# Building gate tables: one multiplication goes to GpSimd, a third of the one-hot rows to VectorE

## The chip, the core and the metric

One core of one Trainium2 chip runs the whole layer in one launch. The metric is the device time of an execution in microseconds; the median of three runs is quoted. The engines are TensorE (PE, with its weight loads as PEld), VectorE (DVE), ScalarE (ACT), GpSimd (POOL) and SyncE (SP, which issues most of the transfers).

## The reference, cut

The kernel computes one layer over 512 tokens of width 1024. An attention group and an RWKV group come first and take the first half of the time; then comes PEER, a product-key retrieval over 128 x 128 = 16,384 single-neuron experts. For each token and each of 8 heads it picks 16 experts, each named by two keys (i1, i2), with a softmax gate:

```python
def block(hb):                       # 128 tokens
    ...
    idx = jnp.take_along_axis(cand_i, pos, axis=-1)          # i1 * 128 + i2
    gate = jax.nn.softmax(top_s, axis=-1).astype(hb.dtype)
    u = expert_u[idx]
    act = jax.nn.gelu(jnp.einsum('thkd,td->thk', u, hb), approximate=False)
    vv = expert_v[idx]
    return jnp.einsum('thk,thkd->td', gate * act, vv)
```

## The kernel before

The 512 tokens are four blocks of 128. Two of them (`GATHERED`, blocks 0 and 3) compute PEER by gathering: in `experts` each of the 128 choices of a token fetches a row of `expert_u` and one of `expert_v` by an indirect DMA that GpSimd issues (L996, 512 KB each), into four buffers `ga`. VectorE takes the dot product (L1006) or accumulates (L1009).

The other two blocks (`DENSE`, 1 and 2, together 256 tokens) compute PEER densely: `dense` goes over all 16,384 experts in 128 tiles. `up` loads a tile of `expert_ut` and multiplies it by the tokens (whole at L1133, or split in two parts and multiplied three times at L1147), with a GELU behind it; `down` multiplies the result by the gate of each token and expert (L1164) and by the tile of `expert_v` (L1168, L1185) into `po`, which stays in PSUM over all 128 tiles.

For this every token needs its gates as a 128 x 128 table over (i2, i1). `make_gates` builds these tables ahead of the loop, in 32 groups of eight tokens. `slots` holds i1, i2 and the gate, the choice (8 heads x 16) on the partitions and the token along the row. Per group:

- `B` (128 x 8 x 128): VectorE compares `iotap` (0 to 127) with i1, which gives one-hot rows (L1061), and multiplies them in place by the gate (L1062).
- `A`, of the same size: one-hot rows of i2. ScalarE computes |i2 - iotap| for each of eight tokens (L1065) and then relu(1 - that) over all eight (L1066).
- TensorE multiplies `A` by `B`, token by token (L1074), into `pg` in PSUM. ScalarE copies a part of it to `G` (L1077), which stays in SBUF, and the rest to `away` (L1078), which SP writes to DRAM every second group.

`B` has two buffers, shared with the later split `xh`, `xl`; `A` has two of its own; `pg` has four. Between two groups the loop in `dense` issues the first tiles of `up`, 16 of them over the 32 groups.

The order on the engines is not that of the source text. A planner with a model of the instructions' times (`schedule_with_timeline_sim=True` at the launch) fills each engine's queue, taking the ready instruction that comes first in the program. So the gates stage runs beside the retrieval of the last block (`back`, `retrieve`, `route`) and beside the gathered rows of `experts`, which stand last in the program and fill in. Once laid out, the order on each engine is fixed, and an instruction waits there for what it needs.

Of the kernel before, what the change touches and what calls it, by code (L numbers as in the profile page):

```python
# [13 lines left out]
AF = mybir.ActivationFunctionType  # L14
OP = mybir.AluOpType
# [3 lines left out]
P = 128  # L19
# [70 lines left out]
def layer_kernel(ctx: ExitStack, tc: tile.TileContext, x, pos, cvec, rvec, w_mla, w_rwkv, w_uq, w_ukv, lora, g2,  # L90
# [20 lines left out]
    mm, act, V, G = nc.tensor.matmul, nc.scalar.activation, nc.vector, nc.gpsimd  # L111
# [26 lines left out]
    def cst(shape, name, dt=F32, pool=pre):  # L138
        return pool.tile(shape, dt, name=name)
# [108 lines left out]
    iotap = cst([P, P], "iotap", pool=con)  # L248
# [14 lines left out]
    for j in range(16):  # L263
# [5 lines left out]
                    op=OP.mult)  # L269
# [26 lines left out]
    def bc(ap, n):  # L296
        return ap[:, :, None].to_broadcast([ap.shape[0], ap.shape[1], n])

    def bm(ap, n):
        return ap[:, None, :].to_broadcast([ap.shape[0], n, ap.shape[1]])  # L300
# [755 lines left out]
    def make_gates(dn, psd, held, far):  # L1056

        i1T, i2T, gT = slots
        for t0 in range(0, nd, 8):
            B = dn.tile([P, D], F32, tag="x", name=f"B{t0}", bufs=XB).rearrange("p (a b) -> p a b", a=8)  # L1060
            V.tensor_tensor(B, bm(iotap, 8), bc(i1T[:, t0:t0 + 8], P), op=OP.is_equal)  # L1061
            V.tensor_tensor(B, B, bc(gT[:, t0:t0 + 8], P), op=OP.mult)  # L1062
            A = dn.tile([P, 8, P], F32, tag="A", name=f"A{t0}", bufs=2)
            for j in range(8):
                act(A[:, j, :], iotap, AF.Abs, scale=-1.0, bias=i2T[:, t0 + j:t0 + j + 1])  # L1065
            act(A, A, AF.Relu, scale=-1.0, bias=1.0)  # L1066
            i = t0 % 16
            if i == 0:
                away = dn.tile([P, D], F32, tag="v", name=f"away{t0}", bufs=VB)
                away = away.rearrange("p (s t i) -> p s t i", s=P // SUB - HELD, i=SUB)  # L1070
            for h in range(2):
                p = psd.tile([P, 512], F32, tag="po", name=f"pg{t0}{h}", bufs=2 * len(DENSE))
                for j in range(4):
                    mm(p[:, j * P:(j + 1) * P], A[:, 4 * h + j, :], B[:, 4 * h + j, :], start=True, stop=True)  # L1074
                p4 = p.rearrange("p (t s i) -> p s t i", t=4, i=SUB)
                t = t0 + 4 * h
                act(held[:, :, t:t + 4, :], p4[:, :HELD], AF.Copy)  # L1077
                act(away[:, :, t % 16:t % 16 + 4, :], p4[:, HELD:], AF.Copy)  # L1078
            if i:
                nc.sync.dma_start(far[:, t0 // 16], away)  # L1080
            yield

    def dense():
# [110 lines left out]
        for i, _ in enumerate(make_gates(dn, psd, held, far)):  # L1194
            for e in range(FIRST + i * rest // n, FIRST + (i + 1) * rest // n):
                up(e, e >= AHEAD)
# [126 lines left out]
```

## Time and profile before

| | |
|---|---|
| median of three runs | 1761.57 us (1759.91, 1761.57, 1781.8) |
| profiled execution | 1773.46 us |
| its span, first to last instruction | 1771.7 us, mean granted TensorE clock 0.926 |
| PE / PEld busy | 1556.0 us (88%) / 1319.3 us (74%) |
| DVE busy | 1358.6 us (77%) |
| ACT busy | 808.1 us (46%) |
| POOL busy | 777.8 us (44%) |
| DMA | 537.52 MB, mean 303 GB/s |

Busy times are sums over the span of one execution. A busy PE is not a PE at its peak, since matrix multiplications are pipelined and their ends are modelled. In rows of instructions, "out<-in" are the program's names without buffer numbers, then partitions x elements and type. A "<-" behind a time of idleness names what ended it; "issue" means that the engine waited for nothing that the profile shows.

### The profile page before, as it was taken

The page shows a single profiled execution, that of the slowest core. Times are in us where ns is not written, and L with a number is a line of the kernel's source. Part 1 is how long each engine was busy: PE and PEld are TensorE (multiplying, and loading weights), DVE is VectorE, ACT ScalarE, POOL GpSimd, SP SyncE. Part 2 cuts the span into 40 slices and gives each one's busy share as a digit, 9 for nine tenths or more (in the row PEclk, how much of TensorE's full clock was granted, in tenths as well). Part 3 has the DMA queues.
Part 4 walks back from the last instruction along what each step waited for, and adds up shares of the span by engine and source line. Part 5 has one row for each costly group of instructions (what it writes and reads, how often), then busy time and mean ns, then how long its engine had stood idle before and what let it go on. Part 6 is the DMA issues. An engine that isn't in the chain of part 4 may idle for free. (4 is left out here: it accounts for less than half of the span.)

```text
span 1771.7 us, 29597 instructions
## 1 busy us (share of the span) xinstructions
PE 1556.0 (88%) x10803; PEld 1319.3 (74%) x10803; DVE 1358.6 (77%) x2788; ACT 808.1 (46%) x2007; POOL 777.8 (44%) x560
## 2 busy tenths in 40 slices
PE   7999998998799897789995668999969999899992
PEld 6896797876575686569985436788868888888872
DVE  3422435678886689988999857898879899898896
ACT  5645634455423422237798302444425444344440
POOL 1001100546674644454437644454445365464574
PEclk9999998998669889899997889999989999999997
DMA  8545644798889889889996899899999999999997
GB/s 279 187 140 189 228 160 129 273 362 275 300 303 385 297 312 322 311 319 359 377 308 209 314 318 347 335 360 345 350 324 367 347 334 364 348 350 364 331 340 274
DMA packets 165617, 537.52 MB, mean 303 GB/s; under 512 B 17824, under 2 KB 32800, under 8 KB 165472
## 3 DMA queue, kind: packets, MB, share of 16 engines
q0 software_dynamic: 73728, 268.47, 42.4%
q1 hardware_dynamic: 91744, 267.17, 42.2%
q8 instruction: 85, 1.39, 0.3%
q14 instruction: 60, 0.49, 0.1%
HBM read 517.34 MB, written 18.22 MB: 302 GB/s over the span
## 5 line engine op out<-in xcount | busy, mean ns | idle before, releaser
L996 POOL DMA_INDIRECT ga<-in_expert_v_dram,idx x235 | 375.8, 1599 | 315.5 <-DVE acc L1009 205.6
L996 POOL DMA_INDIRECT ga<-in_expert_u_dram,idx x225 | 287.5, 1278 | 312.8 <-DVE ga L1006 244.2
L1009 DVE SCALAR_TENSOR_TENSOR acc<-ga,dots,acc 128x1024 f32<-128x1024 f32 x235 | 300.5, 1279 | 33.3 <-DMA ga<-in_expert_v_dram,idx 32.8
L1006 DVE SCALAR_TENSOR_TENSOR ga<-ga,h 128x1024 f32<-128x1024 f32 x225 | 273.6, 1219 | 29.8 <-DMA ga<-in_expert_u_dram,idx 29.1
L1147 PE MATMUL ps<-dh,uh 128*128 128x256 f32 x800 | 231.7, 290 | 24.8 <-ACT uh L1094 24.8
L1147 PE MATMUL ps<-dh,ul 128*128 128x256 f32 x800 | 231.9, 290 | 13.4 <-DVE ul L1095 13.4
L1147 PE MATMUL ps<-dl,uh 128*128 128x256 f32 x800 | 230.5, 288 | 0.0
L1185 PE MATMUL po<-xh,t 128*128 128x512 f32 x544 | 186.1, 402 | 16.1 <-ACT xh L1094 16.1
L1147 PEld LDWEIGHTS ps<-dh,uh 128*128 128x128 f32 x800 | 157.0, 196 | 32.1 <-ACT uh L1094 27.4
L1147 PEld LDWEIGHTS ps<-dh,ul 128*128 128x128 f32 x800 | 156.7, 196 | 19.6 <-DVE ul L1095 17.1
L1147 PEld LDWEIGHTS ps<-dl,uh 128*128 128x128 f32 x800 | 156.8, 196 | 3.1 <-issue 0.5
L1185 PE MATMUL po<-x2h,t 128*128 128x512 f32 x408 | 135.3, 392 | 2.0 <-ACT x2h L1094 2.0
L1094 ACT ACTIVATE xh<-v 128x1024 fp32r<-128x1024 f32 x68 | 71.9, 1057 | 136.3 <-DMA v<-in_expert_v_dram 61.7
L1095 DVE TENSOR_TENSOR ul<-u,uh 128x1024 fp32r<-128x1024 f32 x100 | 121.9, 1220 | 13.6 <-ACT uh L1094 13.5
L1185 PEld LDWEIGHTS po<-xh,t 128*128 128x128 f32 x544 | 101.8, 192 | 39.6 <-ACT xh L1094 19.5
L844 PE MATMUL ps<-h2T,wst 128*128 128x128 f32 (+1 forms) x768 | 125.2, 319 | 4.2 <-DMA wst<-in_w_pq_dram 2.9
L1094 ACT ACTIVATE uh<-u 128x1024 fp32r<-128x1024 f32 x100 | 104.8, 1051 | 43.2 <-DMA u<-in_expert_ut_dram 33.2
L844 PEld LDWEIGHTS ps<-h2T,wst 128*128 128x128 f32 x768 | 110.8, 197 | 12.8 <-DMA wst<-in_w_pq_dram 2.2
L353 PE MATMUL ps<-hT,wst 128*128 128x129 f32 x896 | 110.8, 277 | 0.6 <-ACT t L311 0.6
L1185 PE MATMUL po<-xl,t 128*128 128x512 f32 x272 | 109.8, 404 | 0.7 <-DVE xl L1095 0.5
L1133 PE MATMUL ps<-t,u 128*128 128x256 f32 x448 | 108.0, 395 | 2.7 <-DMA u<-in_expert_ut_dram 2.0
L353 PEld LDWEIGHTS ps<-hT,wst 128*128 128x128 f32 x896 | 105.3, 191 | 6.3 <-issue 1.3
(423 smaller groups left out, 3132.6 us busy)
## 6 DMA issues: line engine op xcount, KB each, us to landing
u<-in_expert_ut_dram SPq DMA_DIRECT2D x128, 512.0 KB, 6.8
v<-in_expert_v_dram SPq DMA_DIRECT2D x128, 512.0 KB, 6.1
wst<-in_w_rwkv_dram SPq DMA_DIRECT2D x56, 512.0 KB, 4.4
wst<-in_w_pq_dram SPq DMA_DIRECT2D x48, 512.0 KB, 6.6
wst<-in_w_o_dram SPq DMA_DIRECT2D x24, 512.0 KB, 6.2
far<-away SPq DMA_DIRECT2D x16, 512.0 KB, 6.1
G<-far SPq DMA_DIRECT2D x16, 512.0 KB, 12.0
wst<-in_w_mla_dram SPq DMA_DIRECT2D x16, 336.0 KB, 6.5
```

Of the source, the lines that this page charges most:

```text
L353: mm(p[:, :P + 1], w[:, kc, :], hT[:, kc, :], start=kc == 0, stop=kc == KC - 1)
L844: mm(p[:, :nb * P], w[:, kc, :], h2T[:, kc, :], start=kc == 0, stop=kc == KC - 1)
L996: G.indirect_dma_start(out=t, out_offset=None, in_=table, in_offset=bass.IndirectOffsetOnAxis(ap=idx[:, j:j + 1], axis=0))
L1006: V.scalar_tensor_tensor(u, u, 1.0, h2, op0=OP.mult, op1=OP.mult, accum_out=dots[:, j:j + 1])
L1009: V.scalar_tensor_tensor(acc, row_of(expert_v, j), dots[:, j:j + 1], acc, op0=OP.mult, op1=OP.add)
L1094: act(hi, t, AF.Copy)
L1095: V.tensor_tensor(lo, t, hi, op=OP.subtract)
L1133: mm(p, u[:, kc, :], hd[kc // 2][:, kc % 2, :], start=kc == 0, stop=kc == KC - 1)
L1147: mm(p, a[:, k, :], h[:, kc, :], start=kc + i == 0, stop=kc == KC - 1 and i == 2)
L1185: mm(po[i][n], ww[:, i * P:(i + 1) * P], vv[:, cols], start=e + k == 0, stop=e == P - 1 and k == 2)
```

## The change

The multiplication by the gate moves from VectorE to GpSimd in all 32 groups. In the groups 2, 5, 8, ... 29 (ten of them) the rows of `A` come from one comparison over all eight tokens on VectorE, in place of nine instructions on ScalarE. What is computed is the same.

```diff
             V.tensor_tensor(B, bm(iotap, 8), bc(i1T[:, t0:t0 + 8], P), op=OP.is_equal)
-            V.tensor_tensor(B, B, bc(gT[:, t0:t0 + 8], P), op=OP.mult)
+            G.tensor_tensor(B, B, bc(gT[:, t0:t0 + 8], P), op=OP.mult)
             A = dn.tile([P, 8, P], F32, tag="A", name=f"A{t0}", bufs=2)
-            for j in range(8):
-                act(A[:, j, :], iotap, AF.Abs, scale=-1.0, bias=i2T[:, t0 + j:t0 + j + 1])
-            act(A, A, AF.Relu, scale=-1.0, bias=1.0)
+            if t0 // 8 % 3 == 2:
+                V.tensor_tensor(A, bm(iotap, 8), bc(i2T[:, t0:t0 + 8], P), op=OP.is_equal)
+            else:
+                for j in range(8):
+                    act(A[:, j, :], iotap, AF.Abs, scale=-1.0, bias=i2T[:, t0 + j:t0 + j + 1])
+                act(A, A, AF.Relu, scale=-1.0, bias=1.0)
```

## Rows read from the trace of the kernel before

**Rows 1.** Windows by stage: stretch, its length, busy us by engine, PEclk, DMA share, GB/s.

```profile
790.00:900.00 110.00, 107.66 (x766) 101.51 (x765) 97.53 (x208) 86.90 (x266) 48.48 (x35) 1.00 0.96 357
900.00:990.00 90.00, 68.51 (x422) 61.57 (x421) 90.00 (x192) 77.66 (x213) 52.86 (x26) 0.85 0.78 258
990.00:1150.00 160.00, 119.88 (x528) 84.78 (x529) 117.54 (x178) 38.74 (x60) 75.06 (x52) 0.88 0.91 331
1150.00:1750.00 600.00, 554.43 (x3326) 491.54 (x3324) 537.00 (x670) 256.86 (x379) 308.98 (x199) 0.98 0.95 348
```

**Rows 2.** Groups, 790 to 990 us: busy us, mean ns; idle before, releasers.

```profile
L996 POOL DMA_INDIRECT ga<-in_expert_v_dram,idx x46 | 83.4, 1813 | 76.0 <-DVE acc L1009 47.2 <-DVE ga L1006 4.8 <-DVE ti L877 3.6
...
L1009 DVE SCALAR_TENSOR_TENSOR acc<-ga,dots,acc 128x1024 f32<-128x1024 f32 x46 | 58.6, 1274 | 3.2 <-DMA ga<-in_expert_v_dram,idx 3.2
...
L1061 DVE TENSOR_TENSOR B<-iotap,slots 128x1024 f32<-128x1024 f32 x32 | 38.8, 1215 | 7.0 <-PE pg L1074 7.0
L1062 DVE TENSOR_TENSOR B<-B,slots 128x1024 f32<-128x1024 f32 x32 | 38.7, 1213 | 0.1
...
L1006 DVE SCALAR_TENSOR_TENSOR ga<-ga,h 128x1024 f32<-128x1024 f32 x16 | 19.5, 1218 | 2.2 <-DMA ga<-in_expert_u_dram,idx 2.1
L996 POOL DMA_INDIRECT ga<-in_expert_u_dram,idx x15 | 18.2, 1216 | 23.1 <-DVE ga L1006 9.2 <-DVE ti L824 4.7 <-DMA ga<-in_expert_v_dram,idx 4.4
```

**Rows 3.** Waits, 900 to 990 us: who for whom, total us, times, longest.

```profile
POOL ga L996 <- DVE acc L1009: 21.2, 16, 4.3
...
PEld pg L1074 <- ACT A L1066: 6.2, 4, 2.4
```

**Rows 4.** Timeline, late in the stage: start, us, engine, instruction, idle before.

```profile
978.96 1.21 DVE L1062 TENSOR_TENSOR B<-B,slots 128x1024 f32<-128x1024 f32 x1
979.31 1.69 POOL L996 DMA_INDIRECT ga<-in_expert_v_dram,idx  x1 [0.65 <-DVE acc L1009]
980.10 1.27 DVE L1009 SCALAR_TENSOR_TENSOR acc<-ga,dots,acc 128x1024 f32<-128x1024 f32 x1
```

**Rows 5.** Timeline of ScalarE: one group's rows of A.

```profile
822.06 2.44 ACT L1065 ACTIVATE A<-iotap,slots 128x128 f32<-128x128 f32 x8
...
825.08 1.06 ACT L1066 ACTIVATE A<-A 128x1024 f32<-128x1024 f32 x1
```

**Rows 6.** Groups of GpSimd over the whole span, shapes apart.

```profile
L306 POOL TENSOR_TENSOR gnr<-gnv,mhalf 128x8 f32<-128x8 f32 x4 | 7.0, 1760 | 14.0 <-DVE gnv L304 14.0
L306 POOL TENSOR_TENSOR onr<-onv,mhalf 128x8 f32<-128x8 f32 x4 | 6.9, 1713 | 64.7 <-DVE onv L304 64.6
...
L616 POOL MEMSET t<- 64x512 f32 x8 | 4.2, 530 | 0.0
...
L306 POOL TENSOR_TENSOR nxr<-nxv,mhalf 128x1 f32<-128x1 f32 x4 | 2.3, 578 | 16.2 <-DVE nxv L304 16.1
```

**Rows 7.** Timeline: an issue while VectorE sits idle.

```profile
805.63 0.95 POOL L996 DMA_INDIRECT ga<-in_expert_u_dram,idx  x1 [0.30 <-issue]
...
807.86 1.23 DVE L1061 TENSOR_TENSOR B<-iotap,slots 128x1024 f32<-128x1024 f32 x1 [3.35 <-PE pg L1074]
```

**Rows 8.** Timeline: an issue during a run of VectorE instructions.

```profile
971.77 4.56 POOL L996 DMA_INDIRECT ga<-in_expert_v_dram,idx  x1 [0.65 <-DVE acc L1009]
972.03 1.21 DVE L1062 TENSOR_TENSOR B<-B,slots 128x1024 f32<-128x1024 f32 x1
973.16 2.35 DVE L1095 TENSOR_TENSOR ul<-u,uh 128x1024 fp32r<-128x1024 f32 x2
```

**Rows 9.** A small power on GpSimd: its durations (ns, min/median/max), and one in time.

```profile
L306 POOL TENSOR_TENSOR mlr<-mlv,mhalf x4: 697/788/1513, 38.4 to 546.1; 128x2 f32<-128x2 f32 x4
...
545.74 1.28 DVE L1009 SCALAR_TENSOR_TENSOR acc<-ga,dots,acc 128x1024 f32<-128x1024 f32 x1
...
546.09 1.51 POOL L306 TENSOR_TENSOR mlr<-mlv,mhalf 128x2 f32<-128x2 f32 x1
```

**Rows 10.** Tile B: durations of the comparison (ns, min/median/max), first and last start.

```profile
L1061 DVE TENSOR_TENSOR B<-iotap,slots x32: 1198/1212/1237, 791.8 to 981.3; 128x1024 f32<-128x1024 f32 x32
```

## The prediction

> **What bounds the kernel now.** I read the windows by stage first [rows 1]. The change touches one stage only, from about 790 to 990 us, in which `make_gates` runs its 32 groups among three other streams: the last block's retrieval, the gathered rows of `experts`, and the first expert loads. In the first 110 us of it TensorE is busy 107.7 us and the DMA engines 0.96 of the time; VectorE has 12.5 us free and ScalarE 23 us. In the last 90 us VectorE is busy for all 90.00 us, while the DMA share falls to 0.78, TensorE works 68.5 us and ScalarE 77.7. So the first part is held by TensorE and transfers, and the second by VectorE alone. After 990 us the DMA share is 0.91, then 0.95 for 600 us: the tables' bytes have to come in anyway, so what this stage can give back is the DMA time it leaves unused, (0.95 - 0.78) x 90 us = 15 us.
>
> Second, the groups of instructions in the stage [rows 2]. VectorE's 187.5 us (97.5 + 90.0) are mostly instructions over 128x1024 elements with two SBUF inputs: 46 accumulations (58.6 us), 32 comparisons (38.8), 32 multiplications (38.7), 16 dot products (19.5), together 156 us or 83%. GpSimd carries 61 gather issues, 101.6 us (83.4 + 18.2), and sat idle 99.1 us before them, most of it until VectorE freed a `ga` buffer.
>
> Third, the waits of the second part [rows 3]: GpSimd's gathers wait for the accumulation L1009 (21.2 us, 16 times), and TensorE's `pg` for ScalarE's `A` (6.2 us). The first says that VectorE's pace is the gathers' pace; the second is all that faster `A` rows could give here.
>
> **The change part by part.** *VectorE gives up 32 multiplications.* In the order of time one such instruction moves the next start by 1.14 us (978.96 to 980.10 [rows 4]; the 1.21 us shown overlap the next). 32 x 1.14 = 36.5 us less, 18.2 us of it in the second part, where half of the groups lie.
>
> *VectorE gains ten comparisons* (the groups with t0 // 8 % 3 == 2: 2, 5, ... 29). They have the shape and operands of L1061, so the same 1.14 us: +11.4 us, half of it, 5.7, in the second part. VectorE net without anything else: -25 us, -12.5 in the second part.
>
> *ScalarE gives up* ten times eight L1065 (8 in 2.44 us, [rows 5]) and one L1066 (1.06): 35 us. I cost this at nothing: ScalarE is not the engine that is full in either part, and the work that hides it is VectorE's. If VectorE became free, the gain would be some of the 6.2 us wait.
>
> *GpSimd gains 32 multiplications over 128x1024 with two SBUF inputs.* The trace has no such row; the nearest stand in [rows 6]. From below: a MEMSET of 512 elements, which only writes, takes 530 ns, 1.04 ns an element; one pass over 1024 is then 1.06 us. From above: the `pow` takes 578 ns for one element and 1,713 to 1,760 for eight, 0.16 us an element, which would be 165 us for 1024. A multiplication is plain streaming, nearer to the MEMSET than to a power; if its two inputs come one after the other it is two passes, 2.1 us, and with a start of its own I take 2.2. In all 70 us. GPSIMD Engine Reference, section Performance versus the Vector engine, of the Trainium skill gives 4,497 ns for an addition over 2048, from which I estimate 2.25 us here and 72 us in all; no run here shows it yet.
>
> *What they cost VectorE.* GpSimd cannot read SBUF while VectorE runs an instruction with two SBUF inputs. An issue takes 0.95 us beside an idle VectorE [rows 7] and 1.69 us started in a comparison or multiplication: that at 979.31 ends at 981.00, 0.83 us after L1062 ended [rows 4]. In a run of such instructions it stands through several: 4.56 us from 971.77, across L1062 and two splits [rows 8]. A `pow` of two elements, 0.70 us at best, took 1.51 beside an accumulation [rows 9]. VectorE in turn was never stretched: L1061 lies between 1198 and 1237 ns [rows 10]. But all that GpSimd read so far were a few numbers. So the bounds for VectorE are 0 and the whole 2.2 us per multiplication. One reader at a time is what the rows show from one side; I take it for both, thus the full hold, for the share of multiplications that meet two-input work: 83% of VectorE's time now, (156 - 38.7 + 12.1) / (187.5 - 26.6) = 80% then; because a held instruction also blocks the short ones behind it, I take 0.85. 32 x 2.2 x 0.85 = 60 us, 30 in each part.
>
> The Trainium skill, SBUF — State Buffer, section Who interferes with whom, states this for both sides: whichever begins first has the shared reads for its whole instruction and the other stands still. The waiting of GpSimd agrees (1.69 against 0.95 us); the waiting of VectorE no row shows. By rows alone, with nothing held, the sum would be -12.5 us; by the page it is the +22 below.
>
> *Queues.* On GpSimd the multiplication stands among gather issues in one order. Behind it wait gathers, and for them the accumulations; in front of it may stand a gather that waits for its buffer. `B` has two buffers, and a group passes every 200/32 = 6.25 us, so a delay of some 6 us between comparison and matrix multiplication is covered; beyond that `pg` is late, then `G` and the next comparison. The multiplication issues no DMA and no queue of SP is passed.
>
> *Sum.* First part: VectorE -18.2 + 5.7 + 30 = +17.5 us, of which its 12.5 free us take all but 5. Second part: the same +17.5, nothing free. Together +22 us. GpSimd then needs 101.6 + 32 x (2.2 + 0.7 wait) = 194 us of 222: close to full, not over. I pass the +22 on one to one, since the order on every queue is fixed and transfers are what comes after. The profiled execution took 1773.5 us (span 1771.7), 12 us or 0.7% above the median 1761.6; the terms are differences read from it, so 1761.6 + 22 = 1784 us.
>
> **The rivals.**
>
> *GpSimd's reads slip in between (faster side).* VectorE's own rows were never stretched [rows 10], which speaks for it; that those reads were tiny speaks against. Then the second part loses 12.5 us and the first nothing, as TensorE and DMA hold it: 1749 us. This decides if a hold costs under (36.5 - 11.4) / 32 = 0.8 us per multiplication. More than the 15 us of unused DMA time can't come back, so even this stays within 2%.
>
> *GpSimd becomes the bound (slower side).* Place: its queue in this stage. If each multiplication must stand as long as the issue at 971.77 (4.56 - 0.95 = 3.6 us) before it reads, then 32 x 5.8 = 186 us, plus 61 issues of at least 0.95 + 0.3 us from one to the next (76 us, [rows 7]) make 262 us against 200: +62, 1823 us. It decides from a wait of (200 - 76) / 32 - 2.2 = 1.7 us, between the two rows. For it: the second part has just such runs of VectorE work. Against: with multiplications gone and accumulations waiting, the runs get shorter.
>
> *The stretch is hidden.* From 990 to 1150 us VectorE is busy only 117.5 of 160 us and DMA 0.91 [rows 1]. If the next stage takes up (0.95 - 0.91) x 160 = 6 us, and the first part all of its 17.5, about +10 remain: 1770 us.
>
> *The order shifts.* The program is laid out by a planner with its own durations (`schedule_with_timeline_sim`). If multiplications take the places of 70 / 3.3 = 21 gathers (61 in 200 us: one per 3.3), 21 x 0.52 MB at 348 GB/s come 32 us later in the dense loop: 1794 us, on the same side as the forecast and within its range.
>
> **How the numbers follow.** Forecast, +10 to +35 us, with the shifted order in it: 0.42. Nothing held, 1745 to 1760: 0.25. Hidden, 1760 to 1772: 0.12. GpSimd the bound, over 1797: 0.21. 2% is 35 us (1726 and 1797), about what a measurement of this kernel can tell from no change; so faster 0.04 (only out of the first rival, by a better order), slower 0.22, within 0.74. The time is that of the likeliest, 1784; its own range is 1772 to 1797. The range for 8 in 10 takes in the no-hold case and a good part of the full queue: 1746 to 1815.
>
> **What would show it.** Right: comparisons and accumulations of the stage with maxima of about 3.4 us (1.2 + 2.2) where a multiplication runs; a GpSimd row of 2 to 4 us x32; the stage ending near 1010 instead of 990 us; GpSimd busy 85% in it. No hold: L1061 stays at 1.21 us and the stage ends by 980. Full queue: GpSimd near 100%, VectorE idle until `B` or `ga`. The price would be wrong if the GpSimd row without a wait were far from 2.2 us; the whole would be wrong if the stage's length and the total moved apart.

## The result and the profile after

The changed kernel takes 1789.2 us (median of six runs, 1780.3 to 1790.9) against 1764.3 us for the kernel before in the same comparison: 1.0106 times as long, with a 95% interval of 1.0069 to 1.0143, or 12 to 25 us more. Its profiled execution has a span of 1788.7 us, 17.0 more than before. The two executions did not reach the edited stage at the same time: the first comparison into `B` starts at 791.8 us before and at 787.1 after. From there to the end the changed kernel takes 1001.6 us against 979.9, 21.7 more.

Groups of instructions from 787 to 1002 us, the gates stage of the changed kernel (busy us, mean ns; idle before, releasers):

```profile
L1062 POOL TENSOR_TENSOR B<-B,slots 128x1024 f32<-128x1024 f32 x32 | 72.9, 2282 | 7.7 <-DVE B L1061 7.3
L1077 PE MATMUL pg<-B,A 128*128 128x128 f32 x512 | 72.1, 297 | 27.2 <-POOL B L1062 27.2
...
L1009 DVE SCALAR_TENSOR_TENSOR acc<-ga,dots,acc 128x1024 f32<-128x1024 f32 x40 | 71.1, 1778 | 4.9 <-DMA ga<-in_expert_v_dram,idx 4.8
...
L1061 DVE TENSOR_TENSOR B<-iotap,slots 128x1024 f32<-128x1024 f32 x32 | 43.9, 1379 | 8.5 <-PE ps L958 2.9 <-PE ps L922 2.9 <-POOL B L1062 2.3
...
L1006 DVE SCALAR_TENSOR_TENSOR ga<-ga,h 128x1024 f32<-128x1024 f32 x15 | 23.3, 1556 | 5.2 <-DMA ga<-in_expert_u_dram,idx 5.2
```

Against [rows 2], VectorE's two-input instructions have become longer where nothing in them changed: the accumulation 1778 ns on average instead of 1274, the dot product 1556 instead of 1218, the comparison 1379 instead of 1215. And a wait has grown: TensorE sat idle 27.2 us before `pg` for a `B` that GpSimd had not finished; before, it was 4.3 us, for VectorE's multiplication.

How one such instruction looks, in the order of time (start, us, engine, instruction):

```profile
940.98 4.52 POOL L1062 TENSOR_TENSOR B<-B,slots 128x1024 f32<-128x1024 f32 x1
941.45 1.22 DVE L1061 TENSOR_TENSOR B<-iotap,slots 128x1024 f32<-128x1024 f32 x1
...
943.78 2.80 DVE L1009 SCALAR_TENSOR_TENSOR acc<-ga,dots,acc 128x1024 f32<-128x1024 f32 x1
945.55 3.78 PE L1077 MATMUL pg<-B,A 128*128 128x128 f32 x16 [6.17 <-POOL B L1062]
...
949.13 1.06 PE L922 MATMUL ps<-t,identb 128*128 128x128 bf16 x8
...
949.44 1.23 DVE L1061 TENSOR_TENSOR B<-iotap,slots 128x1024 f32<-128x1024 f32 x1 [2.86 <-PE ps L922]
```

The multiplication starts at 940.98 and stands while VectorE runs instruction after instruction; it gets its turn at about 943.6 (945.50 less the 1.9 us that it takes undisturbed). The accumulation that starts at 943.78 then takes 2.80 us instead of 1.27: it is held. TensorE waited 6.17 us for this `B`, and VectorE, free and unable to use it, waited 2.86 us for TensorE before its next comparison at 949.44. That comparison writes into the buffer of `B` that the late `pg` reads until 949.33 (945.55 + 3.78). The profile names the small matrix multiplications of `route` (L922) as what ended the wait, but they run on to 950.19, so the buffer is the likelier cause.

The windows that answer to the first two of [rows 1]:

```profile
790.00:900.00 110.00, 103.37 (x742) 97.48 (x743) 99.44 (x174) 71.50 (x212) 87.48 (x50) 1.00 0.91 327
900.00:990.00 90.00, 61.69 (x360) 54.41 (x358) 82.02 (x184) 57.63 (x160) 70.12 (x34) 0.85 0.65 217
```

The DMA share fell from 0.96 to 0.91 and from 0.78 to 0.65; at 327 instead of 357 GB/s and 217 instead of 258 that is 3.3 and 3.7 MB less. That is what arrives at the end. Up to 1020 us the changed kernel had moved fewer bytes, so more were left; packets and bytes after 1020 us, first of before, then of after (the mean is over a window that runs on past the end, and is not used):

```profile
DMA packets 75967, 256.22 MB, mean 309 GB/s; under 512 B 7933, under 2 KB 15397, under 8 KB 75916
```

```profile
DMA packets 78017, 262.94 MB, mean 317 GB/s; under 512 B 8131, under 2 KB 15880, under 8 KB 77966
```

6.72 MB more, at the 2.93 us per MB that the kernel before took for the rest ((1771.7 - 1020) / 256.2), are 19.7 us; the spans differ by 17.0.

### The profile page after: what moved, and what is told of

Read it like the earlier page. It is cut to its first block, busy times and chain, and to the rows that moved or that the text cites. A ratio compares the mean times of both kernels' runs of the same rounds, so it can differ in the third digit from the quotient of the medians.

```text
span 1788.7 us, 29569 instructions
## 1 busy us (share of the span) xinstructions
PE 1557.6 (87%) x10803; PEld 1317.1 (74%) x10803; DVE 1374.7 (77%) x2766; ACT 777.0 (43%) x1917; POOL 836.6 (47%) x592
## 3 DMA queue, kind: packets, MB, share of 16 engines
q8 instruction: 85, 1.39, 0.3%
## 5 line engine op out<-in xcount | busy, mean ns | idle before, releaser
L996 POOL DMA_INDIRECT ga<-in_expert_v_dram,idx x235 | 363.4, 1546 | 335.5 <-DVE acc L1009 241.2
L1009 DVE SCALAR_TENSOR_TENSOR acc<-ga,dots,acc 128x1024 f32<-128x1024 f32 x235 | 320.8, 1365 | 34.9 <-DMA ga<-in_expert_v_dram,idx 34.2
L1006 DVE SCALAR_TENSOR_TENSOR ga<-ga,h 128x1024 f32<-128x1024 f32 x225 | 278.7, 1243 | 37.0 <-DMA ga<-in_expert_u_dram,idx 36.7
L1188 PE MATMUL po<-xh,t 128*128 128x512 f32 x544 | 188.2, 407 | 14.1 <-ACT xh L1097 11.5
L1150 PEld LDWEIGHTS ps<-dh,ul 128*128 128x128 f32 x800 | 158.8, 199 | 22.6 <-DVE ul L1098 20.2
```

The source lines that it names most:

```text
L996: G.indirect_dma_start(out=t, out_offset=None, in_=table, in_offset=bass.IndirectOffsetOnAxis(ap=idx[:, j:j + 1], axis=0))
L1006: V.scalar_tensor_tensor(u, u, 1.0, h2, op0=OP.mult, op1=OP.mult, accum_out=dots[:, j:j + 1])
L1009: V.scalar_tensor_tensor(acc, row_of(expert_v, j), dots[:, j:j + 1], acc, op0=OP.mult, op1=OP.add)
L1150: mm(p, a[:, k, :], h[:, kc, :], start=kc + i == 0, stop=kc == KC - 1 and i == 2)
L1188: mm(po[i][n], ww[:, i * P:(i + 1) * P], vv[:, cols], start=e + k == 0, stop=e == P - 1 and k == 2)
```

## The experiments

### The disputed cost by itself

A small kernel in place of the layer: VectorE and GpSimd run multiplications alone, together, and beside other kinds of work.

> The disputed cost by itself; the layer is left out, the kernel only copies x to the output beside seven stretches. L44: eight VectorE multiplications over 128x1024 with two SBUF inputs, alone. L47: six GpSimd multiplications of that size, alone. L50 with L52: both together. L55 with L57: GpSimd only fills (MEMSET, 1024 elements). L60 with L62: VectorE has one input (a scalar multiplication). L65 with L67: VectorE's second input lies in PSUM, 512 elements. L70 with L72: ScalarE copies. Mutual hold: alone 1.14 us from start to start on VectorE and 1.9 on GpSimd; together 8 x 1.14 + 6 x 1.9 = 20.5 us, with single VectorE rows of about 1.2 + 1.9 = 3.1 us; beside the fills and with the input in PSUM VectorE's rows as when alone. One-sided hold (only GpSimd waits): VectorE's rows stay at 1.21 us in all stretches, and GpSimd's rows are longer by up to 9 us. No hold: 11.4 us together, both as when alone.

Durations in ns, min/median/max, of each stretch:

```profile
L44 DVE TENSOR_TENSOR vo<-x,x x8: 1224/1226/1226, 6.6 to 15.4; 128x1024 f32<-128x1024 f32 x8
...
L47 POOL TENSOR_TENSOR go<-gin,x x6: 2339/2339/2340, 18.0 to 30.1; 128x1024 f32<-128x1024 f32 x6
...
L50 DVE TENSOR_TENSOR vo<-x,x x8: 1225/3244/3246, 33.7 to 54.6; 128x1024 f32<-128x1024 f32 x8
...
L52 POOL TENSOR_TENSOR go<-gin,x x6: 3199/3200/3378, 33.7 to 50.3; 128x1024 f32<-128x1024 f32 x6
...
L55 DVE TENSOR_TENSOR vo<-x,x x8: 1224/1226/1226, 57.2 to 66.0; 128x1024 f32<-128x1024 f32 x8
...
L60 DVE TENSOR_SCALAR vo<-x x12: 693/1702/2711, 68.6 to 88.7; 128x1024 f32<-128x1024 f32 x12
...
L65 DVE TENSOR_TENSOR vo<-x,pp x12: 686/687/689, 90.9 to 98.8; 128x512 f32<-128x512 f32 x12
```

Alone, 1226 ns on VectorE and 2339 on GpSimd. Together, 3244 and 3200: the two take turns, each standing still for most of the other's instruction (VectorE 2.0 of 2.3 us, GpSimd 0.9 of 1.2), and the eight VectorE instructions last 22.2 us instead of 10.0. Beside GpSimd's fills (L55), which write only, VectorE is not touched, nor with its second input in PSUM (L65). Beside ScalarE's copies GpSimd keeps its time (2339 to 2360 ns). The mutual hold is shown; the one-sided hold and no hold fall. The scalar multiplication (L60) has one SBUF input and is held all the same, up to 2711 ns for 693.

This is the rule of the Trainium skill, SBUF — State Buffer, section Who interferes with whom, and the trace now agrees on both sides (3244 against 1226 ns, 3200 against 2339), on the fills and on the PSUM input, and on the scalar instruction, which the page counts among those that can take both ports. That each stands still for the whole instruction agrees only nearly: 2.0 of 2.3 us and 0.9 of 1.2.

### Each part alone

```diff
-            V.tensor_tensor(B, B, bc(gT[:, t0:t0 + 8], P), op=OP.mult)
+            G.tensor_tensor(B, B, bc(gT[:, t0:t0 + 8], P), op=OP.mult)
```

> One part alone: the multiplication on GpSimd in all 32 groups, the rows of A all from ScalarE as before. Hold theory: VectorE loses 36.5 us of work and is stretched by about 43 us as in the changed kernel, so the stage is as long as there or shorter by a part of the ten comparisons (11 us): 1775 to 1790 us, some 0.5 to 1.4% over the kernel before. Rival (the comparisons on VectorE did the harm): as before or faster, 1750 to 1765. Rival (ScalarE's relief was hiding more): over 1795.

1778.9 us, 1.0068 times the kernel before (1.0039 to 1.0098). VectorE's busy time rose by 14.1 us (1372.7 against 1358.6) although 38.7 us of it had gone: 52.8 us of stretch, 1.65 us per multiplication and more than the 43 expected.

The ten comparisons alone, with the multiplication on VectorE:

```diff
+            if t0 // 8 % 3 == 2:
+                V.tensor_tensor(A, bm(iotap, 8), bc(i2T[:, t0:t0 + 8], P), op=OP.is_equal)
+            else:
                 ...
```

> The other part alone: ten groups' rows of A from VectorE, the multiplication on VectorE as before. Hold theory: +11.4 us of VectorE work, half of it in the full part, +6: about 1770 us, ratio 1.00 to 1.006. If the comparisons did the harm: 1780 to 1790. If ScalarE's 35 us counted: 1750 to 1760.

1769.4 us, 0.9998 (0.9978 to 1.0019): nothing, at the lower edge of the hold theory's range. The loss is the multiplication's. Whether the comparisons add something beside it (1.0106 for both, 1.0068 without them) stays open, as the two intervals overlap.

### GpSimd's time kept, its reading taken away

```diff
-            G.tensor_tensor(B, B, bc(gT[:, t0:t0 + 8], P), op=OP.mult)
+            for _ in range(2):
+                G.memset(B, 1.0)
```

> GpSimd's reading taken away and its time kept: in place of the multiplication it fills B twice with ones (2 x about 1 us, the same waits for the comparison in front and the same matrix multiplications behind), so the gate's factor is left out of the tables. Hold theory: the fills read nothing, VectorE's rows stay at 1.2 us, and its 25 us of relief show: 1745 to 1765 us. Queue theory (a GpSimd step of some 2 us between comparison and matrix multiplication, standing among gather issues, is what costs): as the changed kernel, 1780 to 1795 us.

1761.4 us, 0.9963 (0.9937 to 0.9988). The tile B and the accumulations over the whole span:

```profile
L1063 POOL MEMSET B<- x64: 951/952/1962, 788.7 to 965.8; 128x1024 f32 x64
L1061 DVE TENSOR_TENSOR B<-iotap,slots x32: 1205/1220/1229, 785.6 to 960.4; 128x1024 f32<-128x1024 f32 x32
```

```profile
L1009 DVE SCALAR_TENSOR_TENSOR acc<-ga,dots,acc x235: 1240/1280/1361, 419.7 to 1751.0; 128x1024 f32<-128x1024 f32 x118
```

GpSimd has 61 us of new work in the stage, in nearly the same place of its queue, and the kernel is faster than before: no comparison is over 1229 ns and no accumulation over 1361. So the queue theory falls; it is the reading that costs. The planner lays out each kernel anew, so its order is a rival in every comparison of two layers. Here the number of gathers can be counted: 55 of them start between the first comparison and the last `pg`, with the fills as in the changed kernel, against 59 before.

### Twice the multiplications

```diff
             G.tensor_tensor(B, B, bc(gT[:, t0:t0 + 8], P), op=OP.mult)
+            G.tensor_tensor(B, B, bc(gT[:, t0:t0 + 8], P), op=OP.mult)
```

> The changed kernel with the multiplication on GpSimd done twice in every group (the gate enters the tables squared). Hold theory: 32 further instructions of 1.9 us, each of which keeps VectorE's two-input work out, +50 to 61 us of holds with no relief beside them: 1825 to 1850 us, VectorE's accumulations in the stage longer again. Queue theory (only GpSimd's own time counts, and VectorE runs on beside it): GpSimd full in the stage, 1800 to 1825.

1834.5 us, 1.039 (1.0351 to 1.0428), inside the hold theory's range. VectorE's stretch is 89.2 us for 64 instructions (busy 1421.2, against 1358.6 - 38.7 + 12.1), 1.39 us each; in the changed kernel it is 42.7 us for 32, 1.33 each. TensorE's wait for a late `B` grows as well, to 69.3 us from 780 to 1075 us, and the time contains that too.

### The first and the second half of the groups

```diff
-            V.tensor_tensor(B, B, bc(gT[:, t0:t0 + 8], P), op=OP.mult)
+            (G if t0 < nd // 2 else V).tensor_tensor(B, B, bc(gT[:, t0:t0 + 8], P), op=OP.mult)
```

> The multiplication on GpSimd in groups 0 to 15 only, where VectorE still had 12.5 us free; A as before. The prediction's step: +30 of holds - 18 of relief = +12 there, swallowed: 1762 to 1768. If the price is the same everywhere: half of the +0.7% that the multiplication alone cost in all groups, about 1772.

The other kernel has `G` and `V` exchanged.

> The multiplication on GpSimd in groups 16 to 31 only, where VectorE was busy all the time. The prediction's step: +30 - 18 = +12 us, nothing swallows it: 1775 to 1782. If the price is the same everywhere: about 1772.

Measured, the other way round: the first half costs 1.0074 (1.0047 to 1.0100), the second 0.9975 (0.9953 to 0.9997). VectorE was held about as long in both: 22.8 and 24.4 us (busy 1362.0 and 1363.6, with 19.4 us of multiplications gone). Windows 780 to 900 and 900 to 1020 us, of the kernel before, of the first-half kernel and of the second-half one:

```profile
780.00:900.00 120.00, 117.66 (x812) 109.16 (x812) 106.47 (x235) 89.14 (x270) 54.59 (x39) 0.97 0.94 351
900.00:1020.00 120.00, 82.07 (x450) 68.19 (x449) 110.62 (x228) 81.63 (x221) 70.06 (x33) 0.84 0.81 275
```

```profile
780.00:900.00 120.00, 112.19 (x765) 104.78 (x765) 98.86 (x177) 84.21 (x251) 88.12 (x53) 0.96 0.92 328
900.00:1020.00 120.00, 85.77 (x482) 71.25 (x480) 113.96 (x250) 86.64 (x240) 58.79 (x32) 0.87 0.80 269
```

```profile
780.00:900.00 120.00, 117.70 (x829) 110.79 (x828) 108.29 (x250) 97.09 (x294) 58.97 (x41) 1.00 0.97 354
900.00:1020.00 120.00, 67.30 (x361) 56.38 (x359) 111.45 (x180) 70.67 (x188) 84.33 (x51) 0.76 0.78 261
```

In the kernel before, the first of these windows moved 351 GB/s. With the holds in it 328: 2.8 MB less, in the part of the stage in which transfers were nearly full. VectorE is not full there, 98.9 of 120 us, and waits 16.3 us for gathers (5.3 in the kernel before). To see whether the holds or GpSimd's two more microseconds per group delay them, the same kernel with fills in groups 0 to 15:

> Why the first 16 groups cost 0.7% and the last 16 nothing. As the run with the multiplication on GpSimd in groups 0 to 15, but there GpSimd fills B twice with ones (nearly the same GpSimd time, the same waits in front and behind, nothing read; the gate is left out of those tables). If the held reads make the gathers late in the stretch in which transfers are full: as before or faster, 1755 to 1768, with the DMA share from 780 to 900 us back at 0.94 or more. If GpSimd's step of 2 us among the gather issues does it: as that run, 1775 to 1785, DMA share 0.92.

```profile
780.00:900.00 120.00, 117.43 (x827) 110.57 (x825) 88.74 (x203) 96.80 (x293) 83.19 (x71) 1.00 0.98 361
```

1761.6 us, 0.9972 (0.9956 to 0.9987), and 361 GB/s with GpSimd as busy as with the multiplications (83.2 against 88.1 us). The held reads it is. By which path they cost bytes is not isolated. Of what the first-half kernel moved less than the kernel before, two thirds are gathers (19.2 MB on GpSimd's queue against 21.0), but of what it moved less than the kernel with fills only a third (19.2 against 20.5; SP's transfers 20.0 against 22.6). And VectorE waits even longer for gathers with the fills, 27.5 us, so that wait alone is no sign of harm.

Why the second half comes out slightly below 1 is not settled. VectorE's sum there is 24.4 - 19.4 = +5 us. Its profiled execution had 2.0 MB less left at 1020 us than the kernel before, but it was 12 us ahead before the edit acts (first comparison at 779.6 us), and from 780 to 1020 us it moved 73.8 MB against 75.1 before and 71.6 in the first-half kernel. So the holds in the second half seem to cost transfers as well, only fewer. From group 16 on the planner has also laid out another order.

### Relief without GpSimd

```diff
-            V.tensor_tensor(B, bm(iotap, 8), bc(i1T[:, t0:t0 + 8], P), op=OP.is_equal)
-            V.tensor_tensor(B, B, bc(gT[:, t0:t0 + 8], P), op=OP.mult)
+            for j in range(8):
+                V.tensor_scalar(B[:, j, :], iotap, i1T[:, t0 + j:t0 + j + 1], gT[:, t0 + j:t0 + j + 1],
+                                op0=OP.is_equal, op1=OP.mult)
```

> The other way to relieve VectorE, with no GpSimd in it: comparison and multiplication of B become one VectorE instruction per token with two scalars from SBUF (is_equal, then mult; eight over 128x128 per group), A as before. The kernel before shows such scalar instructions at 1.02 us for seven (L932), so eight are 1.16 us against 2 x 1.14: 36 us less VectorE work, as much as moving the multiplication was to give. Hold theory: nothing holds VectorE, so this relief shows as transfers moved earlier, as in the run with fills: 1745 to 1760 us, more bytes between 780 and 1020 us than the 75 MB of before. Rival (VectorE's work in this stage is not what bounds it): 1762 to 1770. Rival (scalar instructions keep GpSimd's gather issues out as the two-input ones do, or more): 1770 to 1785.

1759.8 us, 0.9959 (0.9929 to 0.9990): in the range, with 77.0 MB between 780 and 1020 us instead of 75.1, but not for the reason given. Four of these instructions, of VectorE's timeline, and the gather issues from 780 to 1020 us (ns, min/median/max):

```profile
904.78 1.10 DVE L1062 TENSOR_SCALAR B<-iotap,slots,slots 128x128 f32<-128x128 f32 x4
```

```profile
L996 POOL DMA_INDIRECT ga<-in_expert_v_dram,idx x49: 942/962/3305, 781.1 to 989.1; - x49
```

Four take 1.10 us, 0.25 from start to start, so eight are 2.0 us against 2.28: 8 us of relief, not 36 (VectorE's busy time falls by 5.9). The 0.15 us that I took from L932 was for another form, with constants and a bf16 output. What did improve is GpSimd: an issue takes 962 ns at the median, where the kernel before has 1687 in this window. GpSimd seems to get in sooner between these small instructions with one row as input. That this is where the 7 us come from is inferred, not isolated. It has the lowest ratio of the versions that compute the layer, 1.5% below the changed kernel by the two ratios; its interval overlaps that of the second half.

Both things that had come out below 1 put together (scalar instructions in groups 0 to 15, GpSimd's multiplication in 16 to 31):

> What helped, put together: in groups 0 to 15 B from the scalar instructions with two scalars on VectorE, in groups 16 to 31 the comparison on VectorE and the multiplication on GpSimd; A as before. If the two gains add up: half of 0.41% and 0.25%, ratio about 0.9955, 1755 to 1762. If the gain of the run with groups 16 to 31 was only another order of the program: 0.998 to 1.002.

1771.5 us, 1.0014 (0.9991 to 1.0038). The gains do not add. Which of the two is lost, and whether the order takes it, is not shown.

### One account for all

The bytes left at 1020 us against the span, over all kernels of the layer, each in its one profiled execution. The last two columns count from the first instruction that writes `B`:

| kernel | MB left at 1020 us | span, us | us per MB after it | first `B` at, us | from there to the end, us |
|---|---|---|---|---|---|
| fills in all groups | 249.1 | 1756.2 | 2.96 | 785.6 | 970.6 |
| fills in the first half | 252.6 | 1757.2 | 2.92 | 782.2 | 975.0 |
| GpSimd in the second half | 254.2 | 1754.7 | 2.89 | 779.6 | 975.1 |
| scalar instructions | 255.6 | 1766.0 | 2.92 | 795.8 | 970.2 |
| before | 256.2 | 1771.7 | 2.93 | 791.8 | 979.9 |
| scalar, then GpSimd | 256.9 | 1770.7 | 2.92 | 789.3 | 981.4 |
| comparisons alone | 257.6 | 1772.6 | 2.92 | 784.5 | 988.1 |
| GpSimd in the first half | 258.5 | 1776.4 | 2.93 | 787.9 | 988.5 |
| multiplication alone | 259.8 | 1776.1 | 2.91 | 783.8 | 992.3 |
| both, the change | 262.9 | 1788.7 | 2.92 | 787.1 | 1001.6 |
| multiplication twice | 269.9 | 1823.4 | 2.98 | 782.0 | 1041.4 |

The time per MB stays within 2.89 and 2.98, a spread of 3% or some 22 us of the 750 that follow. So the bytes left sort large differences and not those of a few us: the second-half kernel ends before the one with fills, with 5 MB more left. Part of the bytes is also decided ahead of the edit. GpSimd's order up to the first comparison is the same in all these kernels, and 327.9 to 328.3 MB are left there in each, but the executions reach it up to 16 us apart. Counted from there, the changed kernel takes 21.7 us more than the one before, the multiplication alone 12.4, the doubled one 61.5 and the fills 9.3 less. This agrees with the ratios of the medians within 9 us; the comparisons alone agree least (8.2 us more, where the ratio has none).

With these limits, what the stage does to the time is mostly what it leaves untransferred, and its own length says little: with the multiplication alone it ends later (the last `pg` at 1014 us) than with both parts (1001 us), in a kernel that is no slower. The planner has put 66 gathers into that stage, against 55 with both parts.

## Why the prediction was right, and where it was not

*The forecast* was +22 us by the mutual hold; measured were 12 to 25, the spans +17. The mechanism, that GpSimd's reads hold VectorE, is shown by the probe, by the fills and by the doubled multiplication. That the size came out so near is in part luck, as two steps of the sum were wrong in opposite directions.

*The price on GpSimd*, 2.2 us, is 1.9 us where nothing is in its way (minimum 1891 ns) and 2.28 on average with the waits, 72.9 us in all against the 70 taken. With a full second input the probe has 2.34, near the page GPSIMD Engine Reference, section Performance versus the Vector engine, of the Trainium skill, whose figure gave an estimate of 2.25; the gate's row, one number for 128 elements, is cheaper. Two passes agrees with what a fill of the size takes, 0.95 us.

*The hold* was sized at 60 us and is 42.7. At 1.9 us for each multiplication the share comes to 0.70, so 0.85 was too high. VectorE also waits, for gathers and for TensorE, and a multiplication that falls into such a gap holds nothing; that this makes the difference is argued, not isolated.

*The free time of the first part* was to swallow 12.5 us. This step failed: with the multiplication moved in the first half alone nothing was swallowed, and the kernel took 0.74% more. VectorE's free time there was no slack. Of it 7.0 us stood before comparisons, for `pg`, and 5.3 before dot products and accumulations, for gathers [rows 2], and both depend on what VectorE has finished before: a held dot product (1909 ns on average from 780 to 900 us of that kernel, instead of 1218) hands its `ga` buffer back later, and the next gather can start later. The halves one by one put the cost into the first part; in the changed kernel itself both parts lost about as many bytes (3.3 and 3.7 MB), so how it divides there is not shown. This mistake and the oversized hold had opposite signs: 60 - 25 - 12.5 = 22 was forecast, and VectorE's sum came to 42.7 - 26.6 = +16 us with nothing swallowed.

*That `B`'s two buffers cover the delay* failed too. Some 6 us were to be covered, from groups 6.25 us apart. In the example above the comparison of the late `B`, started at 937.65, ends at 938.86, the multiplication first waits 2.1 us behind a gather and then takes 4.52, and `pg` starts 6.7 us after the comparison. The next comparisons came at 941.45 and 949.44, the first only 3.8 us after the one at 937.65, and the second waited 2.86 us for its buffer. That is what the prediction said of a longer delay, and left out of its sum. TensorE waited 27.2 us in all for `B`; how much of the 17 us that makes is not isolated.

*The second part and the pass-through.* In the changed kernel VectorE's +16 us and the time agree, but passing such a sum on one to one is no rule: the first half had +3 us and cost 13, the second +5 and gained 4, the comparisons alone +12 and cost nothing, the fills -23 and gained 6.5. What passes on is nearer to bytes than to the stage's end. The stage grew by 18 us (791.8 to 988.3 before, 787.1 to 1001.4 after), which fits by chance; the run with the multiplication alone shows that length and total can part.

*The comparisons and ScalarE's 35 us* were costed at +6 and 0; alone they measure 0.9998.

*The rivals.* No hold fell with the probe; without reads the kernel gains 0.4%, some 6.5 us, less than the 12.5 that rival gave. GpSimd as the bound did not come: it is busy 157.6 of the 200 us from 790 to 990. Its worst wait, 2.6 us (4.52 less 1.9), is rare: two of the 32 multiplications take over 4 us. The shifted order is there in a small way: 55 gathers between the first comparison and the last `pg` instead of 59. By the prediction's own price for such gathers that is some 6 us; the fills, with 55 as well, did not pay it.

## What to carry to other kernels

Before moving elementwise work from VectorE to GpSimd, list what VectorE runs beside it: if those are instructions with two SBUF inputs, the move doesn't share the load, it largely serialises the two engines: here 1.2 us of VectorE became 1.9 of GpSimd and 1.3 to 1.65 of stretch on VectorE. An engine's free time in a stage is no slack when it consists of waits for transfers and results that its own instructions release. Where the kernel ends on transfers, compare two versions by the bytes left, not by when the edited stage ends, and count both from the start of that stage, since executions can reach it at different times.

## What was not expected of the hardware

A VectorE instruction with one SBUF input and a constant, over 1024 f32 elements, is held by GpSimd's reads like one with two (693 to 2711 ns), while the same kind over 128 elements with scalars from SBUF let gather issues through (median 962 ns instead of 1687). A GpSimd multiplication by eight numbers, each repeated 128 times, is 19% shorter than one by a full second input (1.90 against 2.34 us).
